# Token rows 1056 elements apart and projection weights stored by even and odd rows, in a hybrid attention and convolution decoder layer

## The chip, the cores and the metric

The kernel runs on one core of one Trainium2 chip. Its metric is the device time of one execution in microseconds (us), the median of three runs. Profiles are of one execution, taken by the hardware profiler; its own time is given beside its span. Engines are named as the profile names them: PE is the matmul engine, PEld its loading of weights, DVE is VectorE, ACT is ScalarE, POOL is GpSimd, SP the queue from which most DMAs are issued.

## The reference, cut to what matters

One layer of a decoder over 1040 tokens (16 meta tokens ahead of 1024), 1024 features wide, all in float32:

```
h  = layer_norm([meta, x])                              # 1040 x 1024
z  = h @ w_in + b_in                                    # 1024 -> 512 q, 128 k, 128 v, 1024 conv, 2048 gates
a  = sliding window attention(q, k, v) @ w_attn_proj    # 512 -> 1024
c  = silu(layer_norm(conv31(c_val * sigmoid(c_gate)))) @ w_conv_proj   # 512 -> 1024
h1 = layer_norm(alpha * h + (sigmoid(g_attn) * a + sigmoid(g_conv) * c) @ w_out)
up = conv3(h1 @ ffn_w_up)                               # 1024 -> 5632
out = layer_norm(alpha * h1 + (gelu(g) * u) @ ffn_w_down)              # 2816 -> 1024
```

## The kernel before, in words

**Split products.** Every large product is made of float32r matmuls in which each operand is the sum of a high and a low part: a high part is a rounded copy (ScalarE, L300), the low part the rest (VectorE, L303). Three matmuls stand for one: weight low by row high (L338), weight high by row high (L341), weight high by row low (L342), all into one PSUM tile. PE's weights are 128 x 128 blocks, and the moving operand is a row of tokens: 128 features on the partitions, 256 to 384 tokens along the free axis.

**Where the operands lie.** The normed tokens are kept as eight rows (one for each 128 features, index k) of 1040 tokens, high parts in the buffer RHO, low parts in RHC. Row k begins at k x 1040 elements (T = 1040), and `h0(k, hl, a, b)` cuts tokens a to b out of it. A weight tile holds the blocks for all eight k, high and low: it is 2304 elements long; the high block of k begins at k x 144 elements (WS = 144), the low block at 1136 + k x 144. Two such tiles (pool wsp) are used in turn. `chunks` makes the two views, `weights` loads and splits a tile. The attention's output (OA, rows given by `oo`) and the convolution's output (OC, rows given by `conv`) have four rows each, again 1040 elements apart, the low parts 4224 elements behind the high ones.

**The stages.** (1) The tokens are loaded, normed, turned and split, with the first three weight tiles (key, value, first query tile) in between; these are written out in a fixed order in `z_first` (L556), in widths of 258 or 272 and 384 tokens. (2) `z_tile` runs the other 27 weight tiles of w_in, each in four groups of tokens (`z_group`): the first 272 wide for the convolution's tiles and 258 wide for query and gate tiles (these start at token 14), the other three 256 wide, 24 matmuls a group. Convolution tiles and three query tiles come first; then the attention over 128-token blocks runs, with gate and convolution tiles placed between its matmuls and the 31 taps of the convolution (L725) on VectorE; the rest of the gate tiles follows, while the convolution's layer norm is worked out (sums over channels by PE at L955, then L993 to L1030). (3) The merge: eight weight tiles (`branch`, `merge`) with four k of attention output and four of convolution output, token groups of 258, 256, 256 and 256, 12 matmuls a group and branch (ps_p). (4) The output projection (ps_w), the up projection (L1534, with seven products in the place of eight for each pair of quadrants), the down projection (L1679).

The up projection's operands lie elsewhere: blocks of 260 or 256 elements per k, weights in unbroken runs of 512, from `W_FLAT` in the two wsp tiles and from a ring in RHO.

**What sets the order.** Each engine executes in the order of its instruction stream. The order is set when the kernel is built, by priorities (`rank`, `RK_...`) and by dependencies that only order (`after`). PE runs ahead of its data only as far as the three PSUM tiles of the tag "mm" allow; ScalarE and VectorE empty them.

Of the kernel before, what the change touches and what calls it, by code (L numbers as in the profile page):

```python
# [24 lines left out]
R = mybir.dt.float32r  # L25
AF = mybir.ActivationFunctionType
OP = mybir.AluOpType
AX = mybir.AxisListType

P = 128  # L30
D = 1024
KC = D // P
NMETA = 16
S = 1024
T = S + NMETA
# [24 lines left out]
HW = 514  # L60
SUB = [(0, 258), (258, HW)]

WS = 144

BS = [260, 256]

LO = 4224
OA_OO, OA_WO, OA_UP = 6, 120, 0
OC_CV, OC_UP = 6, 40
RX_WO = 16  # L70
W_AT = (0, 1136)
W_FLAT = (96, 1136 + 112)
R_DN = 112


# [37 lines left out]
def tile_hybrid_layer(  # L113
# [3 lines left out]
    nc = tc.nc  # L117
# [12 lines left out]
    def f32(ap):  # L130
        return ap.bitcast(F)
# [17 lines left out]
    wsp_p = ctx.enter_context(tc.tile_pool(name="wsp", bufs=2, side="left"))  # L149
# [3 lines left out]
    arena = ctx.enter_context(tc.tile_pool(name="arena", bufs=1, side="left"))  # L153
    dpool = ctx.enter_context(tc.tile_pool(name="scratch", bufs=1, space=bass.MemoryType.DRAM))

    FA = arena.tile([P, 6144], F, name="FA")
    RHC = arena.tile([P, KC * T], R, name="RHC")
    RHO = arena.tile([P, KC * T], R, name="RHO")
    OB = arena.tile([P, 4 * U], F, name="OB")

    v1d = dpool.tile([NH, J_LEN], F, name="v1d")
# [18 lines left out]
    start = ExitStack()  # L180
    sp = start.enter_context(tc.tile_pool(name="start", bufs=1, side="right", reuse_waits="tile"))
# [93 lines left out]


    def h0(k, hl, a, b):
        return (RHO, RHC)[hl][:, k * T + a:k * T + b]

    gb = sp.tile([P, 2, D], F, name="gb")  # L280
    load(gb[:, :, :].rearrange("p a b -> p (a b)"), dram(ln0_in, 0, [[0, P], [1, 2 * D]]))
# [17 lines left out]
    def split(raw, hi, lo, behind=None):  # L299
        ins = nc.scalar.copy(hi, raw)  # L300
        if behind is not None:
            after(ins, behind)
        return nc.vector.tensor_tensor(lo, raw, f32(hi), OP.subtract)  # L303

    def chunks(t):
        return [t[:, o:o + KC * WS].rearrange("p (k c) -> p k c", k=KC)[:, :, :P] for o in W_AT]

    def wsp(dtype=R):
        return wsp_p.tile([P, 2 * KC * WS], dtype, name="w", tag="w")

    def wsp_flat(dtype=R):
        t = wsp(dtype)
# [3 lines left out]
    last_fill, last_split, z_last = [], [], []  # L316

    def weights(shape, fill):
        fills[0] += 1
        n = fills[0]  # L320
        own = n == 3
        raw = OB[:, 0:D].rearrange("p (k c) -> p k c", k=KC) if own else wraw(shape)
        with rank({1: 14, 2: 13, 3: 16, 4: 23}.get(n, RK_SPLIT)):
            last_fill.append(fill(raw))
        hi, lo = chunks(sp.tile([P, 2 * KC * WS], R, name="w3") if own else wsp())
        if n <= 3:
            return hi, lo, raw
        with rank(RK_SPLIT):
            last_split.append(split(raw, hi, lo))
            if n == 7:  # L330
                after(last_split[-1], cin_done[-1])
        return hi, lo

    def product(ps, terms, behind=None):

        n = len(terms)
        for i, (ah, al, bh, bl) in enumerate(terms):
            ins = nc.tensor.matmul(ps, al, bh, start=i == 0, stop=False)  # L338
            if i == 0 and behind is not None:
                after(ins, behind)  # L340
            nc.tensor.matmul(ps, ah, bh, start=False, stop=False)  # L341
            last = nc.tensor.matmul(ps, ah, bl, start=False, stop=i == n - 1)  # L342
        return last

    def z_group(wt, g, a, b, evac):
        hi, lo = wt
        ps = pat.tile([P, 512], F, name="ps_z", tag="mm", bufs=3)
        last = product(ps[:, :b - a], [(hi[:, k], lo[:, k], h0(k, 0, a, b), h0(k, 1, a, b)) for k in range(KC)],
                       z_last[-1] if z_last else None)
        z_last.append(last)  # L350
        with rank(RK_EVAC):
            evac(g, a, b, ps[:, :b - a])
        return last
# [66 lines left out]
    V = nc.vector  # L420
# [105 lines left out]
    first = [weights([P, KC, P], in_cols(m)) for m in (4, 5, 0)]  # L526
    evacs0 = [k_evac, v_evac, q_evac(0)]

    def whigh(i):
        ac(nc.scalar.copy(first[i][0], first[i][2]))  # L530

    def wlow(i):
        hi, lo, raw = first[i]
        last_split.append(dv(V.tensor_tensor(lo, raw, f32(hi), OP.subtract)))

    sums0 = {}

# [4 lines left out]
    def z_first(g, tiles, *ks, raw=False):  # L542

        for i in tiles:
            a, b = span(i, g)
            if ks[0] == 0:
                sums0[i] = pat.tile([P, 512], F, name="ps_z", tag="mm", bufs=3)[:, :b - a]
        for k in ks:
            for i in tiles:
                a, b = span(i, g)  # L550
                hi, lo, w = first[i]
                if raw:
                    pe(nc.tensor.matmul(sums0[i], w[:, k], tms[g, k][:, a - HG[g][0]:], start=k == 0, stop=k == KC - 1))
                    continue
                for j, (w, hl) in enumerate(((lo, 0), (hi, 0), (hi, 1))):
                    ins = nc.tensor.matmul(sums0[i], w[:, k], h0(k, hl, a, b), start=k + j == 0,  # L556
                                           stop=k == KC - 1 and j == 2)
                    if j == 0:
                        pe(ins)
                    pe_done.append(ins)  # L560
# [100 lines left out]
    for a, b in ((0, 400), (400, J_LEN)):  # L661
        ps = pat.tile([P, 512], F, name="ps_v", tag="o" if a == 0 else "t", bufs=1 if a == 0 else 2)
# [24 lines left out]
    V = ap.tile([P, NB, NKV, 2, HD], R, name="v")  # L687
# [52 lines left out]
    ins = load(vd, dram(v1d, 0, [[0, P], [J_LEN, NH], [1, J_LEN]]))  # L740
# [17 lines left out]
    for g in range(NKV):  # L758
# [3 lines left out]
        for lo in (0, 64):  # L762
            for o, i in ((Kx[g][lo:, :, 16:144], kr[lo:, 16:T].rearrange("p (n c) -> p n c", c=P)),
                         (Kx[g][lo:, :, 0:16], kr[lo:, 0:16].unsqueeze(1).to_broadcast([P - lo, NB, 16]))):
                if lo == 0:
                    ins = nc.vector.tensor_copy(o, i)
                else:
                    ins = nc.vector.tensor_tensor(o, i, f32(o), OP.subtract)
# [11 lines left out]
    for q4 in range(2):  # L780
        ps = pat.tile([P, 512], F, name="ps_v4", tag="t", bufs=2)
        for i in range(4):
            c = NMETA + (q4 * 4 + i) * P
# [168 lines left out]
    for g, (a, b) in enumerate(UG):  # L952
# [6 lines left out]


    late = ctx.enter_context(tc.tile_pool(name="late", bufs=1, side="right", reuse_waits="tile"))
    OC = late.tile([P, 8376], R, name="OC")
    oa_stack = ExitStack()
    OA = oa_stack.enter_context(tc.tile_pool(name="oa", bufs=1, side="left", reuse_waits="tile")).tile(
        [P, 8376], R, name="OA")
    tmp_stack = ExitStack()
    tmp_p = tmp_stack.enter_context(tc.tile_pool(name="tmp", bufs=1, side="right", reuse_waits="tile"))

# [4 lines left out]


    def conv(c, hl, a, b):
        o = OC_CV + c * T + hl * LO
        return OC[:, o + a:o + b]

    pinned = []
# [50 lines left out]


    def oo(r, hl, a, b):
        o = OA_OO + r * T + hl * LO
        return OA[:, o + a:o + b]

    def o_split(g, r):
# [91 lines left out]
    for m in range(KC):  # L1128
        hi, lo = weights([P, KC, P], lambda raw: load(raw, w_ab[m]))

        def branch(i, g, tag, bufs):
            a, b = PG[g]
            ps = pat.tile([P, 512], F, name="ps_p", tag=tag, bufs=bufs)
            rhs = (oo, conv)[i]
            product(ps[:, :b - a], [(hi[:, 4 * i + k], lo[:, 4 * i + k], rhs(k, 0, a, b), rhs(k, 1, a, b))
                                    for k in range(4)])
            return ps[:, :b - a]

        def merge(g, psa, psb):
            a, b = PG[g]  # L1140
            n = b - a
            with rank(RK_EVAC):
                t = gslot()[:, :, :n]
                ins = load(t, dram(sgd, m * P * U + a, [[U, P], [KC * P * U, 2], [1, n]]))

                ta, tb = t[:, 0], t[:, 1]
                nc.vector.scalar_tensor_tensor(ta, ta, 1.0, psa, OP.add, OP.mult)
                nc.vector.scalar_tensor_tensor(tb, tb, 1.0, psb, OP.add, OP.mult)
                nc.vector.tensor_tensor(ta, ta, tb, OP.add)
                if g == 0:  # L1150
                    nc.scalar.mul(pair[:, m, 0:2], ta[:, 0:2], 0.5)
                    nc.vector.scalar_tensor_tensor(pair[:, m, 2:4], ta[:, 0:2], 0.5, f32(pair[:, m, 0:2]),
                                                   OP.mult, OP.subtract)
                v = ta[:, n - 256:].rearrange("p (t x) -> p t x", t=2)
                h = mixed2(g, m, 0)
                last_act = nc.scalar.mul(h, v, 0.5)
                nc.vector.scalar_tensor_tensor(mixed2(g, m, 1), v, 0.5, f32(h), OP.mult, OP.subtract)
            return ins, last_act

        if m < KC - 1:  # L1160
            for g in range(4):
                last_gate, last_act = merge(g, branch(0, g, "mm", 3), branch(1, g, "t", 2))
        else:
            pa = [branch(0, g, "mm", 3) if g < 3 else branch(0, g, "s", 2) for g in range(4)]
            for g in range(4):
                last_gate, last_act = merge(g, pa[g], branch(1, g, "t", 2))
        if m in (2, 3):
            raw = (FA[:, 4112:5136], OB[:, 3072:4096])[m - 2]
            load(raw, w_out_v[m + 2])
            prep_wo(m + 2, raw, last_act)  # L1170
        if m < 4:
            early.append(FA[:, E_AT[m]:E_AT[m] + 1024])
            after(load(early[m], w_out_v[m]), last_gate)
# [659 lines left out]
```

## Time and profile before

| | us |
|---|---|
| median of three runs | 1266.63 |
| the runs | 1265.53 to 1266.91 |
| the profiled execution | 1267.56 |
| its span, first to last instruction | 1265.8 |
| PE busy | 1251.5 |
| VectorE busy | 1073.6 |
| ScalarE busy | 592.5 |

In the profile a group row gives the line, the engine, the operation, output and inputs with their shapes, the count, then total busy us, the mean ns of one, and idle time ahead of them. Matmuls overlap: each is shown longer than it holds PE up, so two successive starts in the timeline tell more than one duration. A row of the timeline is: start in us, us from there to the end of the last instruction in the row, the engine, what it is, and xN when N like instructions stand together. A row of a table of stretches is: from and to in us, their length, then busy us of an engine with its instruction count, the granted clock of PE, the share and rate of DMA.

### The profile page before, as it was taken

Reading aid. Unit: us, or ns where it says so; the run is one execution under the profiler, and the core shown is the slowest. Engines: PE = TensorE matmul, PEld = TensorE weight load, DVE = VectorE, ACT = ScalarE, POOL = GpSimd, SP = SyncE. Lnnn points to the kernel's source line nnn. Section 1 sums busy time; section 2 is a strip of 40 time slices with the busy share of each in tenths; the row PEclk is TensorE's granted clock in tenths of the full one; section 3 lists DMA queues with packets and bytes.
Section 4 is the critical chain, followed back from the end, with each engine's and each line's share of the span. In section 5 each row is a group of like instructions: output and inputs, shape, how many; then the busy total and the mean of one; then the engine's idle time right before and its main releaser. Section 6 shows DMA issues by size and latency. Waiting matters only on the chain.

```text
span 1265.8 us, 23035 instructions
## 1 busy us (share of the span) xinstructions
PE 1251.5 (99%) x9186; PEld 1183.6 (94%) x9186; DVE 1073.6 (85%) x1854; ACT 592.5 (47%) x1095; POOL 8.1 (1%) x9
## 2 busy tenths in 40 slices
PE   8999999999999999999999999999999999999997
PEld 7999999999999999788899999999999998888886
DVE  7888999999978476548899999998889887896697
ACT  7532355655473223335665555554455544445330
POOL 0000000001000000000000000000000000000000
PEclk9999999999999999999999999999999999999999
DMA  6375643332438364222145555453454567998712
GB/s 254 103 256 144 178 111 97 105 92 80 124 90 218 111 181 126 84 84 84 67 139 198 198 184 210 165 209 126 159 205 169 192 218 254 389 360 326 267 66 83
DMA packets 98701, 212.19 MB, mean 168 GB/s; under 512 B 11411, under 2 KB 38611, under 8 KB 98338
## 3 DMA queue, kind: packets, MB, share of 16 engines
q1 hardware_dynamic: 84474, 199.64, 47.3%
q10 hardware_dynamic: 14120, 11.08, 2.8%
q8 instruction: 72, 1.18, 0.4%
q14 instruction: 35, 0.29, 0.1%
HBM read 150.29 MB, written 62.70 MB: 168 GB/s over the span
## 4 chain that ended last, share of the span: by engine, by line
PE 87%; DVE 7%; DMA 3%; ACT 2%; issue 1%; SPq 0%; DVEq 0%; ACTq 0%
PE px L1534 12%; PE ps_x L1679 9%; PE ps_z L338 8%; PE ps_z L342 8%; PE py L1534 8%; PE ps_z L341 8%; PE ps_z L1679 5%; PE pz L1534 4%; PE pw L1534 4%; PE ps_p L342 2%; PE ps_p L338 2%; PE ps_p L341 2%; PE ps_w L342 2%; PE ps_w L338 2%; PE ps_w L341 2%; PE ps_z L556 2%
## 5 line engine op out<-in xcount | busy, mean ns | idle before, releaser
L342 PE MATMUL ps_z<-RHC,w 128*128 128x256 f32 (+2 forms) x864 | 244.6, 283 | 0.0
L338 PE MATMUL ps_z<-RHO,w 128*128 128x256 f32 (+2 forms) x864 | 244.3, 283 | 0.2 <-ACT FA L734 0.2
L341 PE MATMUL ps_z<-RHO,w 128*128 128x256 f32 (+2 forms) x864 | 243.1, 281 | 0.0
L338 PEld LDWEIGHTS ps_z<-RHO,w 128*128 128x128 f32 x864 | 162.5, 188 | 2.0 <-ACT FA L705 0.7
L341 PEld LDWEIGHTS ps_z<-RHO,w 128*128 128x128 f32 x864 | 162.6, 188 | 0.7
L342 PEld LDWEIGHTS ps_z<-RHC,w 128*128 128x128 f32 x864 | 162.6, 188 | 0.4
L725 DVE SCALAR_TENSOR_TENSOR FA<-cin,cdw,FA 128x1026 f32<-128x1026 f32 x120 | 152.3, 1279 | 0.7
L1356 DVE TENSOR_TENSOR RHO<-wr,RHO 128x512 fp32r<-128x512 f32 x94 | 63.6, 684 | 7.7 <-ACT RHO L1355 7.5
L1355 ACT CAST RHO<-wr 128x512 fp32r<-128x512 f32 x94 | 56.8, 620 | 25.6 <-DVE wr L1373 12.0
L300 ACT CAST w<-wr 128x1024 fp32r<-128x1024 f32 x37 | 38.7, 1047 | 61.0 <-PE ps_z L342 45.0
L734 ACT ACTIVATE FA<-ps_z,colr 128x258 f32<-128x258 f32 (+1 forms) x64 | 30.2, 473 | 69.5 <-PE ps_z L342 55.3
L1373 DVE TENSOR_TENSOR wr<-wr 128x512 f32<-128x512 f32 x88 | 59.9, 681 | 0.1
L303 DVE TENSOR_TENSOR w<-wr,w 128x1024 fp32r<-128x1024 f32 x37 | 45.1, 1218 | 16.2 <-ACT w L300 14.3
L1546 ACT COPY FA<-px 128x514 f32<-128x514 f32 (+2 forms) x23 | 13.2, 572 | 74.0 <-PE px L1534 74.0
L1356 DVE TENSOR_TENSOR w<-wr,w 128x512 fp32r<-128x512 f32 x60 | 40.5, 684 | 4.9 <-ACT w L1355 4.7
L1534 PE MATMUL px<-OA,RHO 128*128 128x258 f32 x324 | 43.2, 282 | 0.0
L1461 ACT ACTIVATE FA<-OB,coll 128x512 f32<-128x512 f32 x44 | 35.9, 815 | 14.9 <-DVE OB L1542 14.8
L1355 ACT CAST w<-wr 128x512 fp32r<-128x512 f32 x60 | 36.3, 618 | 13.2 <-DVE wr L1373 6.4
L1534 PE MATMUL px<-RHC,RHO 128*128 128x258 f32 (+1 forms) x312 | 41.1, 281 | 0.5 <-ACT OB L1546 0.5
L1534 PE MATMUL px<-OC,RHO 128*128 128x256 f32 x324 | 41.5, 277 | 0.0
L1546 ACT COPY OB<-px 128x514 f32<-128x514 f32 (+2 forms) x46 | 26.2, 569 | 32.2 <-PE px L1534 31.8
L1534 PEld LDWEIGHTS px<-OA,RHO 128*128 128x128 f32 x324 | 40.5, 189 | 0.2 <-ACT OB L1546 0.2
(442 smaller groups left out, 3295.5 us busy)
## 6 DMA issues: line engine op xcount, KB each, us to landing
wr<-in_w_up_dram SPq DMA_DIRECT2D x44, 512.0 KB, 3.6
wr<-in_w_z_dram SPq DMA_DIRECT2D x29, 512.0 KB, 3.7
OB<-in_w_down_dram SPq DMA_DIRECT2D x24, 512.0 KB, 4.9
fd<-FA SPq DMA_DIRECT2D x44, 256.0 KB, 2.1
FA<-sd SPq DMA_DIRECT2D x15, 512.0 KB, 8.7
qt<-qd SPq DMA_DIRECT2D x28, 256.0 KB, 4.1
OB<-td SPq DMA_DIRECT2D x14, 512.0 KB, 9.8
sgd<-FA ACTq DMA_DIRECT2D x48, 128.0 KB, 2.7
```

What stands on the lines that cost most here:

```text
L300: ins = nc.scalar.copy(hi, raw)
L303: return nc.vector.tensor_tensor(lo, raw, f32(hi), OP.subtract)
L338: ins = nc.tensor.matmul(ps, al, bh, start=i == 0, stop=False)
L341: nc.tensor.matmul(ps, ah, bh, start=False, stop=False)
L342: last = nc.tensor.matmul(ps, ah, bl, start=False, stop=i == n - 1)
L725: nc.vector.scalar_tensor_tensor(acc[c], cin[:, j:j + U], wc, acc[c], OP.mult, OP.add)
L1355: nc.scalar.copy(hi, src)
L1356: ins = nc.vector.tensor_tensor(lo, src, f32(hi), OP.subtract)
L1373: ins = nc.vector.tensor_tensor(*x)
L1534: ins = nc.tensor.matmul(o, x[:, ks], bmat(sub, q, hl, k), start=first and k + j == 0, stop=k == 3 and j == 2, skip_group_check=not first)
L1546: copied.append(nc.scalar.copy(*x))
L1679: nc.tensor.matmul(banks[i], l[:, ts], r[:, ws], start=first and a and x + k == 0, stop=z and x == len(ops) - 1 and k == 2, skip_group_che ...
```

## The change

The rows of normed tokens, of attention output and of convolution output begin 1056 elements apart (HP) in the place of 1040. A weight tile is 2112 elements long: the high blocks of even k begin at 0, 128, 256 elements and so on, those of odd k 544 behind them, and the low blocks 1056 behind the high ones. The two splits write through a view with the axes (pair of k, even or odd, column); products pick their block with `at_k`. `W_FLAT`, which cuts two plain rows out of the same tiles in later stages, has new offsets. RHO and RHC are 128 elements longer each, OC 64, OA 48, and a weight tile 192 shorter, so later buffers begin at other addresses; all these moves are multiples of 128 bytes. The instructions of each engine and their order are those of before, but for one wait of the SP queue that stands a few places later.

```
-WS = 144
+HP = 1056
...
-W_AT = (0, 1136)
-W_FLAT = (96, 1136 + 112)
+W_LEN, W_STEP, W_ODD = 2112, 1088, 544
+W_AT = ((0, 0), (1024, 32))
+W_FLAT = (32, 1056)
...
-    RHC = arena.tile([P, KC * T], R, name="RHC")
-    RHO = arena.tile([P, KC * T], R, name="RHO")
+    RHC = arena.tile([P, KC * HP], R, name="RHC")
+    RHO = arena.tile([P, KC * HP], R, name="RHO")
...
     def h0(k, hl, a, b):
-        return (RHO, RHC)[hl][:, k * T + a:k * T + b]
+        return (RHO, RHC)[hl][:, k * HP + a:k * HP + b]
...
     def chunks(t):
-        return [t[:, o:o + KC * WS].rearrange("p (k c) -> p k c", k=KC)[:, :, :P] for o in W_AT]
+        return [t[:, o:o + W_STEP].rearrange("p (e x) -> p e x", e=2)[:, :, x:x + 4 * P].rearrange(
+            "p e (j c) -> p j e c", c=P) for o, x in W_AT]
+
+    def at_k(t, k):
+        return t[:, k // 2, k % 2]
+
+    def by_k(raw):
+        return raw.rearrange("p (j e) c -> p j e c", e=2)
...
     def wsp(dtype=R):
-        return wsp_p.tile([P, 2 * KC * WS], dtype, name="w", tag="w")
+        return wsp_p.tile([P, W_LEN], dtype, name="w", tag="w")
...
-            last_split.append(split(raw, hi, lo))
+            last_split.append(split(by_k(raw), hi, lo))
...
-        last = product(ps[:, :b - a], [(hi[:, k], lo[:, k], h0(k, 0, a, b), h0(k, 1, a, b)) for k in range(KC)],
+        last = product(ps[:, :b - a], [(at_k(hi, k), at_k(lo, k), h0(k, 0, a, b), h0(k, 1, a, b)) for k in range(KC)],
...
-    OC = late.tile([P, 8376], R, name="OC")
+    OC = late.tile([P, 8440], R, name="OC")
...
-        [P, 8376], R, name="OA")
+        [P, 8424], R, name="OA")
...
     def conv(c, hl, a, b):
-        o = OC_CV + c * T + hl * LO
+        o = OC_CV + c * HP + hl * LO
...
     def oo(r, hl, a, b):
-        o = OA_OO + r * T + hl * LO
+        o = OA_OO + r * HP + hl * LO
...
-            product(ps[:, :b - a], [(hi[:, 4 * i + k], lo[:, 4 * i + k], rhs(k, 0, a, b), rhs(k, 1, a, b))
+            product(ps[:, :b - a], [(at_k(hi, 4 * i + k), at_k(lo, 4 * i + k), rhs(k, 0, a, b), rhs(k, 1, a, b))
```

The lines of the first three tiles (`whigh`, `wlow`, `z_first`) change in the same way, with `by_k` and `at_k`.

More of the change, by code (lines that the diff above doesn't have):

```diff
@@ L324, in weights @@
             last_fill.append(fill(raw))
-        hi, lo = chunks(sp.tile([P, 2 * KC * WS], R, name="w3") if own else wsp())
+        hi, lo = chunks(sp.tile([P, W_LEN], R, name="w3") if own else wsp())
         if n <= 3:
@@ L529, in whigh @@
     def whigh(i):
-        ac(nc.scalar.copy(first[i][0], first[i][2]))
+        ac(nc.scalar.copy(first[i][0], by_k(first[i][2])))
     def wlow(i):
         hi, lo, raw = first[i]
-        last_split.append(dv(V.tensor_tensor(lo, raw, f32(hi), OP.subtract)))
+        last_split.append(dv(V.tensor_tensor(lo, by_k(raw), f32(hi), OP.subtract)))
     sums0 = {}
@@ L555, in z_first @@
                 for j, (w, hl) in enumerate(((lo, 0), (hi, 0), (hi, 1))):
-                    ins = nc.tensor.matmul(sums0[i], w[:, k], h0(k, hl, a, b), start=k + j == 0,
+                    ins = nc.tensor.matmul(sums0[i], at_k(w, k), h0(k, hl, a, b), start=k + j == 0,
                                            stop=k == KC - 1 and j == 2)
```

## The prediction

> **What bounds the kernel now.** I read the page first: the busy times and the chain that ended last.
>
> ```profile
> span 1265.8 us, 23035 instructions
> PE 1251.5 (99%) x9186; PEld 1183.6 (94%) x9186; DVE 1073.6 (85%) x1854; ACT 592.5 (47%) x1095; POOL 8.1 (1%) x9
> PE 87%; DVE 7%; DMA 3%; ACT 2%; issue 1%; SPq 0%; DVEq 0%; ACTq 0%
> ```
>
> The kernel is a stream of 9186 matmuls, and 87% of the chain is that stream. A busy PE hides gaps, since a matmul is shown for 280 ns though the next starts 115 ns later. So the view that matters is the timeline of PE, read from start to start. The groups with shapes kept apart say which matmuls the change touches:
>
> ```profile
> L342 PE MATMUL ps_z<-RHC,w 128*128 128x256 f32 x648 | 182.7, 282 | 0.0
> L338 PE MATMUL ps_z<-RHO,w 128*128 128x256 f32 x648 | 181.8, 281 | 0.2 <-ACT FA L734 0.2
> L338 PE MATMUL ps_z<-RHO,w 128*128 128x258 f32 x152 | 43.8, 288 | 0.0
> L338 PE MATMUL ps_z<-RHO,w 128*128 128x272 f32 x64 | 18.7, 292 | 0.0
> L342 PE MATMUL ps_p<-OA,w 128*128 128x256 f32 x96 | 26.8, 279 | 0.0
> L341 PE MATMUL ps_p<-OC,w 128*128 128x256 f32 x96 | 26.6, 277 | 0.0
> L342 PE MATMUL ps_p<-OA,w 128*128 128x258 f32 x32 | 9.1, 284 | 0.0
> L556 PE MATMUL ps_z<-RHO,w 128*128 128x384 f32 x96 | 24.9, 341 | 0.0
> L556 PE MATMUL ps_z<-RHC,w 128*128 128x384 f32 x48 | 16.3, 340 | 0.0
> ```
>
> Three lines (L338, L341, L342) issue each product, as often each, so the projection of the tokens (ps_z) has 3 x 648 = 1944 matmuls of 256 columns, 456 of 258 and 192 of 272; the merge stage (ps_p, six such rows of 96, first and last shown, and six of 32) has 576 of 256 and 192 of 258; the three first tiles (L556) have 144 of 384. All other matmuls keep their operands' places modulo 128 bytes, because every buffer that moves does so by a multiple of 128.
>
> **What the layout does.** With 1040 elements (4160 bytes) between rows and 144 (576 bytes) between weight blocks, both start addresses flip by 64 bytes, modulo 128, from one k to the next. In the built program a 256-column matmul of ps_z has its moving row at residue 32 for even k and 96 for odd k, and its weights at 32 or 96, each block 64 bytes off the row that streams while it is loaded. With 1056 (4224 = 33 x 128 bytes) and weights 512 bytes apart inside the even and the odd half (2176 = 17 x 128 bytes from half to half), every one of the 2520 matmuls of 256 and the 144 of 384 has its row at 32 and its weights at 96; the 258 wide have 24 and 96, the 272 wide 96 and 96. The same residues, 32 against 96, are what the 256-column products of the up stage (L1534) have today. So the trace holds both layouts side by side. First the token projection, the starts of successive groups of 24 matmuls in the timeline of PE:
>
> ```profile
> 92.05 0.29 PE L338 MATMUL ps_z<-RHO,w 128*128 128x272 f32 x1
> ...
> 95.09 0.28 PE L338 MATMUL ps_z<-RHO,w 128*128 128x256 f32 x1
> ...
> 97.87 0.28 PE L338 MATMUL ps_z<-RHO,w 128*128 128x256 f32 x1
> ...
> 100.63 0.28 PE L338 MATMUL ps_z<-RHO,w 128*128 128x256 f32 x1
> ...
> 103.39 0.28 PE L338 MATMUL ps_z<-RHO,w 128*128 128x258 f32 x1
> ...
> 106.27 0.28 PE L338 MATMUL ps_z<-RHO,w 128*128 128x256 f32 x1
> ...
> 109.07 0.28 PE L338 MATMUL ps_z<-RHO,w 128*128 128x256 f32 x1
> ```
>
> A settled group of 256 takes 97.87 to 100.63, 2.76 us, 115.0 ns a matmul. Then the up stage, 12 matmuls to a row:
>
> ```profile
> 660.35 1.54 PE L1534 MATMUL px<-OC,w 128*128 128x256 f32 x12
> 661.73 1.61 PE L1534 MATMUL pw<-OA,w 128*128 128x258 f32 x12
> 663.18 1.53 PE L1534 MATMUL pw<-RHC,w 128*128 128x256 f32 x12
> 664.54 1.61 PE L1534 MATMUL py<-OA,RHO 128*128 128x258 f32 x12
> ```
>
> Here 256 columns take 663.18 to 664.54: 1.36 us for 12, 113.3 ns. The difference, 1.7 ns a matmul, is what the change can take.
>
> **Token projection, 256 columns.** 81 groups (27 tiles by three), 2.76 us against 2 x 1.36 = 2.72: 0.04 us each, 3.24 us.
>
> **Merge stage, 256 columns.** 48 groups of 12, in the timeline 12 matmuls apart:
>
> ```profile
> 424.87 0.28 PE L338 MATMUL ps_p<-OA,w 128*128 128x256 f32 x1
> ...
> 426.25 0.28 PE L338 MATMUL ps_p<-OC,w 128*128 128x256 f32 x1
> ```
>
> 1.38 us each against 1.36: 48 x 0.02 = 0.96 us.
>
> **After a 258-wide group.** The first 256 group then takes 106.27 to 109.07, 2.80 us, 0.04 over the settled one; in the up stage the first 12 after a 258 take 1.36 (above) or 660.35 to 661.73, 1.38, that is 0 to 0.02 over. The gain is 0.02 to 0.04 in 19 places outside the attention (8 merge tiles, 4 projection tiles ahead of it and 7 behind): 19 x 0.03, about 0.5 us.
>
> **384 columns.** At the settled rate, 113.3/256 = 0.443 ns a column, a matmul would take 170 ns; the trace has
>
> ```profile
> 43.24 0.52 PE L556 MATMUL ps_z<-RHO,w 128*128 128x384 f32 x2
> ...
> 46.41 0.51 PE L556 MATMUL ps_z<-RHO,w 128*128 128x384 f32 x2
> ```
>
> 18 matmuls in 3.17 us, 176. Between nothing and 6 ns each; I take the middle, 144 x 3 = 0.4 us.
>
> **258 and 272 columns.** No row shows them at a constant start. 672 of 258 (the first tiles' 24 with them) stand at 103.39 to 106.27, 120 ns with the entry; the straight rate gives 114, the up stage's mixed starts 661.73 to 663.18, 1.45/12 = 121. 192 of 272 stand at 92.05 to 95.09, 3.04/24 = 127; the straight rate gives 120. The gain is at most 672 x 5 + 192 x 7 = 4.7 us; the loss by the up row 0.7, and I double it to 1.4, since that row's starts are not these. Their row and weights keep the distance they have now (72 and 0 bytes), so I take 0.
>
> **Splits of the weights.** ScalarE (L300) and VectorE (L303) keep their order; they write w in 4 x 2 blocks instead of 8. Strides cost nothing today: the write into gapped w takes as long as the one into plain OA.
>
> ```profile
> L300 ACT CAST w<-wr x37: 1031/1049/1053, 48.2 to 513.4; 128x1024 fp32r<-128x1024 f32 x37
> L300 ACT CAST OA<-FA x4: 1043/1046/1050, 501.9 to 504.7; 128x1024 fp32r<-128x1024 f32 x4
> ```
>
> I cost it at 0, bounded by the 3 ns between those medians, 0.1 us over 37 tiles on either side, and if it were more VectorE's slack (below) is what covers it. No DMA changes.
>
> **What is late next.** Up to the end of attention VectorE is nearly full, by the busy times in stretches (projection before attention, then attention):
>
> ```profile
> 58.90:149.70 90.80, 82.29 (x104) 1.00 0.64 187
> 149.70:351.80 202.10, 196.39 (x403) 1.00 0.38 107
> ```
>
> In attention it has 5.7 us of slack in 202, so a PE that is ready earlier will partly wait for scores and transposes. Against that, where the stretch ends VectorE has formed csum and waits for PE's sums of it:
>
> ```profile
> 352.65 1.49 DVE L993 TENSOR_TENSOR FA<-FA,ps_m 128x386 f32<-128x386 f32 x3 [2.40 <-PE ps_m L955]
> ```
>
> 2.40 us of its time is free there, so up to that much can come through. About 63 of the 81 groups lie before it (with the 384s and the entries, 63 x 0.04 + 0.4 + 0.1 = 3.0 us). I let half of it be lost: 1.5.
>
> **Sum.** 3.24 + 0.96 + 0.5 + 0.4 - 1.5 = 3.6 us. The profiled execution took 1267.56 us (1265.8 span, 1.8 around it): 1264.0. The median of the three runs, 1266.63, is 0.9 below it, so I forecast 1263.0.
>
> **Rivals.** Everything comes through: VectorE gives way, the 384s go to 170 and the unequal widths take half their bound: 3.24 + 0.96 + 0.5 + 0.86 + 2.35 = 7.9, 1258.7. For it: 2.40 us free on VectorE; against: 5.7 in 202. 18%.
> Attention keeps it all: of the token projection only the 18 late groups count, 18 x 0.04 + 0.96 + 0.3 = 2.0: 1264.6. 12%.
> Addresses are not the cause, and the 1.7 ns belong to the tile-to-tile switching in the product: no change, 1266.6. Against it is that the up stage switches tiles as often at 113.3. The Trainium skill, "SBUF — State Buffer", section "SBUF: two separate sides", says that only the port pair shared by VectorE and GpSimd causes contention inside the engine side and that PE never waits on anyone; by that rule the place of a row could not matter. The trace disagrees, 115.0 ns against 113.3 for one shape. 11%.
> Slower: at a constant start the unequal widths meet their weights badly at every matmul instead of at some. If the 6.6 ns that 272 columns stand above the straight rate came once more on all 864, that is 5.7 us, and 5.7 - 3.6 = 2.1 more than now: 1268.7. It decides from 3.6/864 = 4.2 ns a matmul. For it: 272-wide groups have row and weights at the same residue, before and after; against: they have had that all along and it costs nothing new. 9%.
>
> **How the numbers follow.** The forecast's case has 50%. A measurement of this kernel can tell about 0.2%, 2.5 us, from no change: below 1264.1 lie the forecast and the large rival, 68%; within it the two small ones, 23%; above it the last, 9%. The range 1258.3 to 1266.2 reaches down over the large rival and up to just short of no change, leaving the last two, 20%, out.
>
> **What would show it.** Right: settled ps_z groups of 256 at 2.72 us and ps_p at 1.36, L1534 unchanged. The 2.40 wait at L993 shrinks by what came through attention. Wrong: 256-wide matmuls still at 115 (addresses are not it), 258 above 124 (the slower case), or the stage ending at 351.80 no earlier though its groups are quicker (VectorE kept it).

## The result: 0.3% slower, and the profile after

The changed kernel takes 1270.64 us (median of 8 runs, 1268.76 to 1271.45), the kernel before 1266.62 on the same chip: a ratio of 1.0031, 95% interval 1.0020 to 1.0041. The forecast was 1263.0. The profiled execution of after took 1270.37 us, with a span of 1268.5. Its page:

```profile
span 1268.5 us, 23035 instructions
...
PE 1255.2 (99%) x9186; PEld 1187.9 (94%) x9186; DVE 1074.0 (85%) x1854; ACT 591.7 (47%) x1095; POOL 8.1 (1%) x9
...
PE 97%; DVE 1%; DMA 1%; ACT 1%; issue 0%; SPq 0%; DVEq 0%
```

PE is busy 3.7 us longer with the same 9186 matmuls, the other engines as before, and PE's share of the chain is larger. No wait was added: the matmuls themselves come at a slower pace. The timeline of PE in after, at the starts of successive groups of 24 in the projection:

```profile
95.54 0.29 PE L346 MATMUL ps_z<-RHO,w 128*128 128x256 f32 x1
...
98.37 0.28 PE L346 MATMUL ps_z<-RHO,w 128*128 128x256 f32 x1
...
101.20 0.28 PE L346 MATMUL ps_z<-RHO,w 128*128 128x256 f32 x1
```

A settled group takes 2.83 us, 117.8 ns a matmul; before it was 2.76, and forecast was 2.72. Some groups take 2.80 (116.7 ns). In the merge, 12 matmuls apart:

```profile
425.86 0.28 PE L346 MATMUL ps_p<-OA,w 128*128 128x256 f32 x1
...
427.27 0.28 PE L346 MATMUL ps_p<-OC,w 128*128 128x256 f32 x1
```

1.41 us against 1.38. Where the 4 us build up shows in the first rows of the up stage and of the down stage, in the timeline of PE before,

```profile
610.24 1.58 PE L1534 MATMUL px<-OC,RHO 128*128 128x256 f32 x12
...
1047.16 5.63 PE L1679 MATMUL ps_z<-OC,RHC 128*128 128x512 f32 x24
```

and after:

```profile
614.38 1.57 PE L1542 MATMUL px<-OC,RHO 128*128 128x256 f32 x12
...
1050.92 5.40 PE L1687 MATMUL ps_z<-OC,RHC 128*128 128x512 f32 x23
```

After is 4.14 us late when the up stage begins, and the stage takes 436.5 us in after and 436.9 before. What was lost was lost ahead of it, in the stretch of projection and merge. After is 3.76 us late at the first row of the down stage and 2.8 at the end: some 27 us into that stage PE lost 1 us in that one execution of before, and not in that of after.

### The profile page after: what moved, and what is told of

It reads as the page before. It is cut to its first block, busy times and chain, and to the rows that moved or that the text cites. A ratio compares the mean times of both kernels' runs of the same rounds, so it can differ in the third digit from the quotient of the medians.

```text
span 1268.5 us, 23035 instructions
## 1 busy us (share of the span) xinstructions
PE 1255.2 (99%) x9186; PEld 1187.9 (94%) x9186; DVE 1074.0 (85%) x1854; ACT 591.7 (47%) x1095; POOL 8.1 (1%) x9
## 4 chain that ended last, share of the span: by engine, by line
PE 97%; DVE 1%; DMA 1%; ACT 1%; issue 0%; SPq 0%; DVEq 0%
PE px L1542 15%; PE py L1542 10%; PE ps_x L1687 9%; PE ps_z L346 8%; PE ps_z L349 8%; PE ps_z L350 8%; PE ps_z L1687 7%; PE pz L1542 5%; PE pw L1542 5%; PE ps_p L346 2%; PE ps_p L349 2%; PE ps_p L350 2%; PE ps_w L350 2%; PE ps_w L346 2%; PE ps_w L349 2%; PE ps_z L564 2%
```

## The experiments

Three readings were open after the result. Theory J: what counts is how far the rows and weights jump from one k to the next, modulo 256 bytes (64 before, 128 after, 0 in the up stage). Theory D: the distance from row to weights, modulo 512. Theory P: the order of the three matmuls of a k. In the built programs the z stage's addresses give these jumps; the residue modulo 128 on which the prediction rests is the same for after and for the up stage.

**A probe (e1).** A kernel of its own that computes nothing of the layer: 110 series of 48 matmuls of 256 columns (some 258, 272, 384), each with its own places of row and weights, run forwards through the list and then backwards; no other engine works meanwhile.

```
def z(m0, dm, rel, ...):    # eight k of three matmuls: the row jumps by dm bytes from k to k,
    ...                     # each weight block lies rel bytes ahead of the row that streams while it is loaded
```

> A kernel of its own: 110 series of 48 matmuls on two small buffers, run forwards and then backwards, with chosen start addresses; it computes nothing of the layer. Theory J (the jump): a matmul's pace is set by how far the start of its row lies, modulo 256 bytes, from where the row before it began, as long as each weight block lies 64 bytes ahead of the row streamed while it loads. Then series at one fixed place and distance 64 settle at 113.3 ns, jumps of 64 a k at 115.0, jumps of 128 at 116.7 to 117.8, jumps of 256 and 512 at 113.3 again. Theory D (the distance): a jump costs nothing by itself, the distance from row to weights decides, modulo 512; then every jump with the distance held at 64 settles at 113.3, and only the series with the addresses of the changed kernel, where the distance is 320 at each change of k, stands at 117.8. Theory P (the order of the parts): the series with the changed kernel's addresses and the high weights first settles at 113.3, like the up stage. In all three the series with the addresses of the kernel before gives 115.0 and that of the changed one 117.8, if these two buffers stand for the kernel.

Measured, the mean time from start to start over the last 24 of a series (two numbers where forwards and backwards differ):

| row and weights jump together, modulo 256 | ns | nothing jumps, distance row to weights | ns |
|---|---|---|---|
| 0 (by 0, 512 and 1024 bytes) | 113.3 | 0 | 119.7, 120.0 |
| 0 (by 256 bytes) | 117.8 | 160 | 120.0 |
| 32 | 115.8, 118.0 | 32 | 118.3 |
| 64 (also 320) | 115.0 | 64 (also 320) | 117.8, 113.3 |
| 96 | 117.2 | 96 | 117.4, 117.3 |
| 128 (also 384) | 117.8 | 128 | 118.8, 118.6 |
| 192 | 117.3 | 192 | 117.8 |

With the layout of before the probe gives 115.0, with that of after 117.8 forwards and 116.7 backwards, with rows of after and weights of before 116.7, with weights of after and rows of before 117.8. The timeline of the probe, for four series (distance 64 without a jump, forwards; jump 64; jump 128; distance 64 without a jump, backwards):

```profile
21.40 6.05 PE L98 MATMUL ps<-RW,WT 128*128 128x256 f32 x50
...
235.87 5.92 PE L98 MATMUL ps<-RW,WT 128*128 128x256 f32 x50
...
247.03 6.06 PE L98 MATMUL ps<-RW,WT 128*128 128x256 f32 x50
...
1302.81 5.85 PE L98 MATMUL ps<-RW,WT 128*128 128x256 f32 x50
```

Fifty matmuls are 49 starts and 0.28 us of the last: 117.8, 115.1, 118.0 and 113.7 ns, the first matmuls of a series with the rest. The probe repeats the pace of both kernels to 0.1 ns with no other engine at work, so neither the other engines nor the order of instructions is needed to explain it. Theory D falls: the jumps cost with the distance held, and the distance repeats every 256 bytes. Theory J is borne out as far as 0, 64 and 128 go, with weights 64 bytes ahead of the row; at other distances nothing reached 113.3 even without a jump. At 256 it missed: the series stood at 117.8 in both directions, between neighbours at 119.0 and 115.0, where 113.3 was expected. Also not expected: the same places, distance 64 and no jump, ran at 113.3 in one direction and at 117.8 in the other, and all that differs is what ran before. Further series of the probe take row and weights apart. A row that jumps by 128 over still weights takes 117.8 and 116.7 ns; weights that jump by 128 under a still row settle at 113.3 both times, and so do weights whose low blocks alone lie 128 bytes off. So a jump of 128 costs as a jump of the row, not of the weights alone; the experiments below move the weights only together with rows that jump.

**Weights alone (e2), high part first (e3).**

```
-HP = 1056
+HP = 1040          # e2: the weights of after, the rows of before
```
```
 # e3, in product: high by high, high by low, low by high
+            ins = nc.tensor.matmul(ps, ah, bh, start=i == 0, stop=False)
...
+            nc.tensor.matmul(ps, ah, bl, start=False, stop=False)
+            last = nc.tensor.matmul(ps, al, bh, start=False, stop=i == n - 1)
```

> The weights by even and odd rows, the token, attention and convolution rows 1040 elements apart as before. Theory J: the rows still jump by 64 bytes a k, so 256-wide groups of 24 stay near 2.76 us if the weights' place does not count, or rise above it since their distance to the rows is no longer always 64. Theory D: the distance now changes with k, 64 or 128 or others, so the groups are slower than the changed kernel's 2.83. Theory P: 2.80 or more, the order of the parts being as before.

> The changed kernel with the three matmuls of a product in the order high weights by high row, high weights by low row, low weights by high row, as the up stage has it. Theory P: groups of 24 at 256 columns fall to 2.72 us, the merge's groups of 12 to 1.36, and the time to about 1262. Theory J: 2.80 to 2.83 as in the changed kernel, and the time within 2 us of 1270.6. Theory D: the distance of 320 comes at another of the three matmuls, 2.80 to 2.83 as well.

Measured, one run each: e2 1270.99 us, e3 1269.68, the kernel before beside them 1267.84. The timeline of e2, 24 matmuls apart:

```profile
97.92 0.28 PE L346 MATMUL ps_z<-RHO,w 128*128 128x256 f32 x1
...
100.74 0.28 PE L346 MATMUL ps_z<-RHO,w 128*128 128x256 f32 x1
```

2.82 us, 117.5 ns: the new weights, under rows that still jump by 64, make the projection as slow as the whole change does. e3 stands at 2.80, so the order of the three is not the cause.

**Other orders of k (e4, e5, e6).** Nothing is moved; the eight k are summed in another order, so that the jumps become fewer.

```
 # e4, in z_group; in the merge (0, 2, 1, 3)
-for k in range(KC)]
+for k in (0, 2, 4, 6, 1, 3, 5, 7)]
 # e5: the order changes from group to group; in the merge ((0, 2, 1, 3), (1, 3, 0, 2))[i]
+for k in ((0, 2, 4, 6, 1, 3, 5, 7), (1, 3, 5, 7, 0, 2, 4, 6))[len(z_last) % 2]]
 # e6: the kernel before with
+for k in (0, 4, 1, 5, 2, 6, 3, 7)]
```

> The changed kernel with the eight k of a projection group summed in the order 0 2 4 6 1 3 5 7, and the four of a merge group in the order 0 2 1 3; nothing lies elsewhere than in the changed kernel. Rows and weights then move by a multiple of 256 bytes from k to k except at two places of a group (inside, and from its end to the next group), where they move by an odd multiple of 128. Theory J (what counts is the jump modulo 256 bytes from one k to the next: 113.3 ns at 0, 117.8 at 128, so 13.4 ns for each jump of 128): a group of 24 takes 24 x 113.3 + 2 x 13.4 = 2.747 us instead of 2.80 to 2.83, a merge group of 12 1.387 instead of 1.413, and the run comes out some 6 to 8 us below the changed kernel, about 1263. Theory H (the probe's two settled states of one and the same placing: a jump throws the stream into the slow state, and it stays there): groups stay at 2.80 to 2.83 us, run 1270. Theory M (my prediction's: residues modulo 128 bytes alone): the order changes nothing, 2.80 to 2.83 us, run 1270.

> The changed kernel with the k of one projection group in the order 0 2 4 6 1 3 5 7 and of the next in the order 1 3 5 7 0 2 4 6, and in the merge 0 2 1 3 for the attention product and 1 3 0 2 for the convolution's; nothing lies elsewhere. One jump of 128 bytes is left in a group, inside it. Theory J: 24 x 113.3 + 13.4 = 2.733 us a group of 24 and 1.373 a merge group of 12; 81 full groups x (2.82 - 2.733) = 7.0 and 48 x 0.04 = 1.9, so some 8 to 9 us below the changed kernel: 1262, and 4 to 5 us below the kernel before, ratio to it 0.996 to 0.997. Theory H: groups 2.80 to 2.83, run 1270, ratio 1.003. If the settling after a jump takes a dozen matmuls rather than one step: 2.76 to 2.78 us, run 1265 to 1267.

> The kernel before with the eight k of a projection group in the order 0 4 1 5 2 6 3 7; nothing lies elsewhere than in the kernel before, and the merge keeps its order. Rows and weights move by 256 bytes and by 64 bytes in turn (modulo 256: 0 and 64) instead of always by 64. Theory J: half of the jumps cost nothing; 24 x 113.3 + 4 x 5.1 = 2.740 us a group of 24 instead of 2.760, run 1.6 us lower, about 1265. Rival W (where the low weights lie against the row counts as much as the jump; here at the row's own residue, where a placing that never moves took 119.7 ns in the probe, and two thirds of the loads are 64 bytes ahead): groups of 2.78 to 2.84 us, run 1268 to 1273.

Measured: e4 1269.38 us and e6 1271.12 (one run each), e5 1267.35, the kernel before 1266.55; e5's ratio is 1.0006 (0.9997 to 1.0016). Groups of 24 take 2.79 us in e4, 2.76 in e5, and 2.78 or 2.86 in e6; merge groups of 12 take 1.43 in e4 (two jumps and less room to settle; after has 1.41) and 1.40 in e5, which is why e5, level with the kernel before in the projection, is not below it. None of the three numbers is theory J's (2.747, 2.733, 2.740), and e6 went to its rival. One group of e5 in the timeline shows why; its jump of 128 comes after the first 12 matmuls:

```profile
96.56 0.28 PE L346 MATMUL ps_z<-RHO,w 128*128 128x256 f32 x1
...
97.92 0.28 PE L346 MATMUL ps_z<-RHO,w 128*128 128x256 f32 x1
...
98.98 0.28 PE L346 MATMUL ps_z<-RHO,w 128*128 128x256 f32 x1
...
99.32 0.28 PE L346 MATMUL ps_z<-RHO,w 128*128 128x256 f32 x1
```

The 12 ahead of the jump take 1.36 us, 113.3 ns each; the nine behind it 1.06, 117.8; the last three 0.34, 113.3 again. From start to start the seven behind the jump read 117, 119, 123, 118, 115, 120 and 118 ns, 37 ns more than seven at 113.3. So a jump of 128 (row and weights together) throws the stream out of step, and it takes seven matmuls to settle: one jump is 37 ns, two are 74 (e4: 24 x 113.3 + 74 = 2.794). In after a jump comes every third matmul, and the stream never settles. Theory J's 13.4 ns a jump was an average over a stream that was always in between. I call what is left theory S: the cost is the settling.

**Nothing jumps (e7, e8).** Rows 1088 elements apart (4352 = 17 x 256 bytes), weights in one piece.

```
-HP = 1056
+HP = 1088
...
-W_AT = ((0, 0), (1024, 32))
+W_AT = (0, 1024)           # e8: (0, 1056)
...
+        return [t[:, o:o + D].rearrange("p (k c) -> p k c", c=P) for o in W_AT]
```

> Rows of tokens, attention and convolution outputs 1088 elements apart (4352 = 17 x 256 bytes) and each k's 128 weights right behind the last k's (512 bytes), high part and low part 1024 elements apart, in the same weight tiles as in the changed kernel: modulo 256 bytes no row and no weight block ever moves, the weights stand 64 bytes ahead of the row. To make room, the scratch of the convolution's layer norm lies in a free part of another buffer, and the sums of the down stage have one buffer instead of two; nothing is left out. Theory S (a group pays for settling after each jump modulo 256 bytes, 37 ns after a jump of 128 as the orders of k showed, and runs at 113.3 ns where nothing jumps): groups of 24 at 2.720 us and merge groups at 1.360, against 2.760 and 1.380 before: 81 x 0.04 + 48 x 0.02 = 4.2 us, and 0.06 for each of the 8 groups of 272: about 4.5 us below the kernel before, 1262, ratio 0.9965 (less what the moved scratch and the single sums buffer cost). Theory H (the probe's second state of this same placing, 117.8 ns): 2.826 and 1.413, about 1270, ratio 1.003. Theory D (the placing matters only through the sum of what each instruction reads): no statement.

> The kernel e7 with the low parts of the weights 1056 instead of 1024 elements behind the high parts: low blocks 128 bytes off modulo 256, high blocks as in e7, as the changed kernel has them within its even and within its odd rows. In the probe this settled at 113.3 both times (the placing of e7 at 113.3 or 117.8, by what came before). Theory S: as e7, groups of 2.720 and 1.360 us, ratio 0.9965. If e7 falls into the slow state and e8 does not, the slow state belongs to the placing with all at one distance; if both do, to what comes before.

Measured: 1320.15 and 1318.48 us (ratios 1.0418, 1.0404 to 1.0433, and 1.0405, 1.0390 to 1.0419). The whole time says nothing of the theories: the layer norm's scratch had to wait for a buffer that the gate tiles use until then, as the waits of e7 show,

```profile
PE ps_p L346 <- DVE OC L1036: 14.9, 1, 14.9
```

and the clock granted to PE was 0.88 of full from 400 to 500 us. Against what was planned, these two leave something out: the one sums buffer is overwritten by raw weights for the last sums of the down stage. So only the projection is read from them. There, ahead of the attention, the settled groups of 24 stand at 2.720 us in both, but for one in e7 at 2.826, and the first group behind a 258-wide one takes mostly 2.738 in e7 and 2.747 in e8. So 113.3 ns is reached in the kernel itself, as theory S has it. Theory H, that one placing has a second, slow pace, shows in e7 too: of the 45 groups of the projection that run without a break (no start over 200 ns behind the last), five stand at 117.8, four of them in the attention. In e8 none of 45 does. The same group in e7,

```profile
165.31 0.28 PE L346 MATMUL ps_z<-RHO,w 128*128 128x256 f32 x1
...
168.14 0.28 PE L346 MATMUL ps_z<-RHO,w 128*128 128x256 f32 x1
```

and in e8:

```profile
164.68 0.28 PE L346 MATMUL ps_z<-RHO,w 128*128 128x256 f32 x1
...
167.42 0.28 PE L346 MATMUL ps_z<-RHO,w 128*128 128x256 f32 x1
```

They take 2.83 and 2.74 us. That is the outcome for which e8's expectation says that the slow pace belongs to the placing with all at one distance. One trace of each shows it, and no run joins e8's weights with the room that the next three find.

**Room for it (e9, e10, e11).** The same placing in the merge too, with the room found elsewhere: the scratch lies where OA comes later, and the raw buffer of the down stage is halved.

```
-    RXF, SM1 = (sums_p.tile([P, 2048], F, name=n) for n in ("raw", "sums"))
+    RXF, SM1 = (sums_p.tile([P, n], F, name=s) for n, s in ((1024, "raw"), (2048, "sums")))
...
-    F_RAW = [RXF[:, 0:1024], RXF[:, 1024:2048]] + ...
+    F_RAW = [RXF[:, 0:1024]] + ...                        # e9
+    F_RAW = [RXF[:, 0:1024], SM1[:, 0:1024]] + ...        # e10: second place, for the first eight loads
+    F_RAW = [RXF[:, 0:1024], FA[:, 5156:6180]] + ...      # e11: u2 moved from FA to OB, FA 64 longer
```

> As e7: rows 1088 elements apart, weight blocks 128 elements apart in one piece, so that modulo 256 bytes nothing moves in the projection and in the merge; the convolution outputs' and the up stage's operands now keep the residues that they have in the changed kernel. Room comes from other places than in e7: the layer norm's scratch lies where the attention outputs' split parts come later, and the down stage has seven raw buffers instead of eight. PE's instructions come in the same order as in the changed kernel. Theory S: projection groups of 24 at 2.720 us and merge groups of 12 at 1.360, the groups of 258 at 2.885 (as in e7) against 2.853 before: 81 x 0.04 + 48 x 0.02 - 20 x 0.03 - 16 x 0.015 = 3.3 us below the kernel before, ratio 0.9974, and 7 us below the changed kernel, if the merge does not start later and the down stage does not wait for its seventh buffer (up to 1 us). Theory H (the slow one of the probe's two states in the merge, where no run has yet shown this placing): merge groups at 1.413, 48 x 0.05 = 2.5 us more, ratio 0.9994.

> The kernel e9 with the raw data of the down stage's second operand loaded into the sums buffer that lies idle at that time (e9 had one buffer fewer there, and PE waited 5.2 us for that load at the entry of the down stage: up to there it was 2.97 us ahead of the kernel before). Theory S: the wait goes, the 2.97 us stay, and the run ends 3 to 4 us below the kernel before (4 if the 0.97 us wait that the kernel before has at that entry goes too): 1262.6 to 1263.6, ratio 0.9969 to 0.9977, and 7 us below the changed kernel. Rival (the entry of the down stage eats what comes early, since its first operands wait for the end of the up stage's sums): ratio 0.999 to 1.000.

> The kernel e9 with a free place of its own for the raw data of the down stage's second operand, made by moving the up stage's intermediate rows within the buffers that hold them (e10 had put it into a sums buffer that came free late, and PE waited 8.9 us there). Rows and weights as in e9: nothing jumps modulo 256 bytes in the projection and the merge. Theory S: 2.97 us ahead of the kernel before at the end of the up stage, as e9, and the entry of the down stage as in the kernel before or without its 0.97 us wait: 1262.5 to 1263.6, ratio 0.9969 to 0.9977, 7 to 8 us below the changed kernel. Rival (the entry of the down stage takes it back, wherever that load goes): a wait of 2 us or more at the first groups of the down stage, ratio 0.999 or above.

Measured: e9 1270.66 us, ratio 1.0037 (1.0024 to 1.0049); e10 1278.18, 1.0093 (1.0076 to 1.0110); e11 1263.30, 0.9974 (0.9964 to 0.9985). The first two miss at one load, e10 by its pace as well. PE's waits of e9,

```profile
PE ps_z L1692 <- ACT OC L1641: 4.3, 1, 4.3
```

and of e10:

```profile
PE ps_z L1694 <- ACT OC L1643: 8.9, 1, 8.9
```

Ahead of this wait e9 had the gain: PE was 2.97 us ahead of the kernel before at the end of the up stage. e9 then had no free place for the second operand of the down stage; e10 gave it one that is in use through most of the up stage, and the wait grew. But e10 was 0.65 us behind the kernel before already when the down stage began. Its rows and weights lie where e9's do, and yet a merge group of e10 takes 1.41 us, where e9's take 1.36:

```profile
425.43 0.28 PE L346 MATMUL ps_p<-OC,w 128*128 128x256 f32 x1
...
426.84 0.28 PE L346 MATMUL ps_p<-OA,w 128*128 128x256 f32 x1
```

From 367 us on every 256-wide group of e10's projection and all 48 of its merge settle at 117.8 ns; e9, slow over the same groups from 367 us, is back at 113.3 from 387 us on, but for the last two groups of the merge. Two kernels with one placing, at two paces: theory H holds, and it took e10 the whole gain. What kept e10 at the slow pace no run tells.

In e11 the wait is gone. Its page and its groups of 24:

```profile
span 1261.8 us, 23039 instructions
...
PE 1248.2 (99%) x9186; PEld 1181.1 (94%) x9186; DVE 1072.9 (85%) x1854; ACT 593.0 (47%) x1096; POOL 8.1 (1%) x9
```

```profile
97.21 0.28 PE L346 MATMUL ps_z<-RHO,w 128*128 128x256 f32 x1
...
99.93 0.28 PE L346 MATMUL ps_z<-RHO,w 128*128 128x256 f32 x1
...
102.65 0.29 PE L346 MATMUL ps_z<-RHO,w 128*128 128x258 f32 x1
```

2.72 us, and 1.36 a merge group. Read from start to start, 83 of the 93 groups of 256 that run without a break settle at 113.3 ns and 10 at 117.8. These 10 begin between 155 and 378 us, in the attention and soon after it, and from 507 us, behind 512-wide matmuls. So the placing alone doesn't decide, and part of the gain is still left. e11 is faster than both kernels: 3.4 us below the one before and 7.3 below the changed one (the kernel before, run beside each of the two, differs by 0.1 us). In the trace it is 2.98 us ahead of the kernel before at the first row of the down stage. e10's pace would cost it 3.6 us; its eight runs lie within 1.5 (1262.70 to 1264.20), so none of them looks like e10.

**Rows alone (e12).** The rows of after with the weights of before, with e11's moves of buffers.

```
 HP = 1056
+WS = 144
+W_AT = (0, 1136)
```

> Rows 1056 elements apart as in the changed kernel, weight blocks 144 elements apart as in the kernel before, with the buffers' moves of e11 to make room (its scratch, raw buffers and intermediate rows): one part of the change alone. Modulo 256 bytes the row now moves by 128 and the weights by 64 from k to k. Theory S (any jump of row or weights modulo 256 bytes keeps PE from settling): as the probe's series of this placing, 116.7 ns, groups of 24 at 2.80 us and merge groups at 1.40; 81 x 0.04 + 48 x 0.02 = 4.2 us above the kernel before in these stages, less the 0.97 us wait at the entry of the down stage that e11 no longer had: 1269 to 1270, ratio 1.0025. Rival (rows and weights moving by the same amount, as in the kernel before and in the changed one, is what a placing is judged by, and the weights' move is what made the changed kernel slow): groups at 2.76, ratio 0.9995.

Measured: 1268.96 us, ratio 1.0020 (1.0010 to 1.0029). Groups of 24 take 2.80 us, merge groups 1.40, as in the probe. So each part of the change, with the other part's jump of 64 left as it was, slows the projection, rows to 116.7 ns and weights to 117.5, and both together are hardly worse than the weights (117.8): the costs don't add. That each keeps the stream from settling is theory S's account of it and not shown step by step; taken for every jump of the weights it is too wide, by the probe's 113.3 ns where weights jump by 128 under a still row.

## Why the prediction was wrong, point by point

**What bounds the kernel.** Right. PE's pace is the time: PE is 4.1 us late when the up stage begins and the run is 4.0 us longer; e11 is 3.0 us ahead at the end of that stage and its run 3.4 shorter. Reading from start to start was needed: by the durations of single matmuls the groups of ps_z differ by 1 to 3 ns of 282.

**What the layout does.** This is the step that failed. It said that residues modulo 128 bytes decide, and that after and the up stage are therefore alike. The evidence was one pair, 115.0 against 113.3, and 128 was only one period that fits it; 256 fits it too, and modulo 256 before jumps by 64, the up stage by 0 and after by 128. By the one reading the change is a gain, by the other it is a layout that no row of before shows. I took the period that made the change do something good and priced a layout as measured that was not: after was to run at the up stage's 113.3 ns, and it runs at 117.8. The probe repeats it with no other engine at work: 64 costs 1.7 ns, 128 costs 4.5.

**Token projection and merge, 256 columns.** Sizes and places were right, the sign was not. Summed from start to start, the 1944 matmuls of ps_z take 3.13 us more than before (forecast 3.24 less, ahead of what attention keeps), the 576 of ps_p 1.17 more (forecast 0.96 less). With rows and weights that really stay in place as the up stage's do, e11, they take 1.97 and 1.03 less.

**Entries, 384, 258 and 272 columns.** The first group behind a 258-wide one takes 2.82 us in after, no less than before (2.80). The 384s gained 0.2 us (forecast 0.4), and 0.3 in e11. For 258 and 272 the forecast was nothing; they changed by 0.15 and 0.21 less over 672 and 192 matmuls. The rival on this side was wrong in its mechanism: after is slower, as it said, but by the 256-wide ones, which it left at 113.3. In e11 the 258-wide ones do lose 0.5 us, well below its 5.7.

**Splits.** Right: the write into the two-way view takes as long as before, in the groups of after:

```profile
L301 ACT CAST w<-wr 128x1024 fp32r<-128x1024 f32 x37 | 38.8, 1049 | 62.5 <-PE ps_z L350 46.1 <-PE ps_p L350 10.4 <-PE ps_z L564 5.4
```

**What is late next.** Half the gain was to be lost in attention, and the 2.40 us wait at L993 to shrink. The wait of that instruction in after,

```profile
355.14 5.14 DVE L1001 TENSOR_TENSOR FA<-FA,ps_m 128x386 f32<-128x386 f32 x12 [2.37 <-PE ps_m L963]
```

is as it was, 2.5 us later. A loss goes through attention: PE was 1.2 us late at its start and 2.5 at this point. A gain does not: e11 was 1.2 us ahead at the start and 1.4 here, though 39 groups' worth of 256-wide matmuls (946) lie between. That is less than half, but what was given for it, VectorE, is only one candidate: there are the groups at the slow pace too (4 of the 10 before 282 us), and no run tells the two apart.

**The rivals.** That addresses are not the cause has fallen for good. The Trainium skill's rule from "SBUF — State Buffer", section "SBUF: two separate sides", that PE waits on no one there, can't be read as saying that PE's pace is the same wherever the operands lie: in the probe, with every other engine idle, it went from 113.3 to 120.0 ns by start addresses alone.

**What would make it wrong** was named with "256-wide matmuls still at 115"; that they could go above 115 was not thought of, and had no rival.

## What to carry to other kernels

Back-to-back matmuls of 256 columns reached their fastest pace here, 113.3 ns, where the row kept its start address modulo 256 bytes and the weights lay 64 bytes ahead of it, and even there not always (e10 ran the merge at 117.8). Row pitches and weight blocks that are multiples of 256 bytes are worth a trial, read by group from start to start; so are low weight blocks 128 bytes off, as in e8, and an order of the contraction in which jumps are rare, since each jump of 128 was paid over the next seven matmuls. A period taken from two layouts is a guess: list every period that fits both, and see whether the new layout is really one of those measured. When space is taken for a better layout, the gain (here 3 us) can be lost many times over to one load that finds its buffer late.

## What the runs showed of the hardware that was not expected

- With nothing else running, a 256-column matmul with its weight load takes 113.3 to 120.0 ns by start addresses and what ran before. Without a jump the pattern over the distance from row to weights repeats every 256 bytes. Of the jumps, 320, 384 and 448 bytes cost what 64, 128 and 192 do, to 0.2 ns; 256 bytes did not repeat 0 (117.8 against 113.3).
- A row that jumps by 128 bytes from k to k over still weights costs 3.4 to 4.5 ns a matmul (116.7 and 117.8), weights that do so under a still row nothing (113.3 ns).
- After one jump of 128 bytes by both the stream needs seven matmuls to settle and loses 37 ns; a change of width from 258 to 256 costs 18 to 27 ns in the same way (2.738 and 2.747 against 2.720 us).
- One and the same placing has two settled paces, 113.3 and 117.8 ns, by what ran before it. e11 has both, 83 groups and 10, and e10, placed the same modulo 256 bytes, has its whole merge at 117.8. What throws the stream from one to the other stays open, and so does what in the chip has the period of 256 bytes.
